# Layer 0 feed-forward by seven block products instead of eight, with narrower PSUM tiles and half-width modulation steps

## The chip, the cores and the metric

The kernel runs on one core of a Trainium2 chip. The metric is the device time of one execution in microseconds, median of several. The core's engines run side by side, each through its own list of instructions in program order: TensorE (PE, matrix products; its weight loads are shown apart as PEld), VectorE (DVE), ScalarE (ACT), GpSimd (POOL) and SyncE (SP, which here only issues transfers). An instruction starts when the one before it on its engine lets it and when what it waits for on other engines or transfers is done.

## The reference, cut to what matters

A two-layer block on 512 latent tokens and 256 context tokens (768 together) of width 1024. Both layers end in the same feed-forward part; its hidden width is 2816, 22 tiles of 128.

```
for i in range(2):
    mod_lat = split((silu_c  @ ada_w[i] + ada_b[i]), 6)     # six vectors of 1024 ("chapters")
    mod_ctx = split((silu_cc @ ada_w[i] + ada_b[i]), 6)
    ...mixer (layer 0: a gated linear recurrence; layer 1: attention over all tokens)...
    x   = x   + mod_lat[5] * swiglu(modulate(rmsnorm(x,   g), mod_lat[3], mod_lat[4]), w_in[i], w_out[i])
    ctx = ctx + mod_ctx[5] * swiglu(modulate(rmsnorm(ctx, g), mod_ctx[3], mod_ctx[4]), ...)   # layer 0 only

def swiglu(h, w_in, w_out):
    g, u = split(h @ w_in, 2)
    return (silu(g) * u) @ w_out
```

## The kernel before

Activations lie with features on the partitions: `hh`/`hl` hold the normalised input as 8 tiles ("k tiles") of 128 features by 768 tokens, latent first. Every matrix product runs three times, since each operand is a rounded high part and a low part (the rest): high·high, low·high, high·low, all into the same PSUM tile.

Weights come through the class `Stream`. SP loads raw tiles of up to 1 MB (two at a time); ACT copies each half of 1024 columns into a high part `wh`, and `low_engine` (DVE in the feed-forward) subtracts to get the low part `wl`. Four such units are kept ahead of TensorE; `st.done(unit)` frees one and lets the next be split.

Layer 0's feed-forward is `ffn(0, ...)`. It takes the 22 hidden tiles in three phases of 8, 8 and 6. For a hidden tile `j` it forms the gate product (`f..g`) and the input product (`f..u`), each over 8 k tiles, three matmuls per k tile, each of these cut into 512 latent and 256 context columns; then ACT takes silu of the gate into `sg`, DVE multiplies (`sg`), ACT and DVE split the result into `ah` and `al`. After a phase's tiles come 8 output tiles (`fo`), added into the residual `xT` by `residual`, one DVE instruction for the latent and one for the context columns. PSUM tiles are three of 1024 columns (`psm`, 2 banks each), from which everything takes turns. The first two tiles' products are interleaved with the norm (`entry`).

Beside it run the modulation steps of layer 1. `ada_step` takes one loaded tile of `ada_w` (128 x 1024, 512 KB, two buffers, loads issued on GpSimd's queue) and adds it on DVE, scaled by silu(c), to a running sum (`ada_sum`; chapters 0 and 1 also for the context, `adac`). After eight of them `ada_add` sums over partitions on TensorE with `pick`, ACT copies (`adasb`), TensorE transposes, DVE adds the bias. All six chapters (48 steps) are done in layer 0's feed-forward, one step after a gate product and one after each tile. `ada_until` does what is missing of a chapter at once.

`boundary` interleaves the last output tiles with the next norm and the first products of layer 1. Layer 1's feed-forward is the same function with 512 columns, and has no modulation steps left.

Of the kernel before, what the change touches and what calls it, by code (L numbers as in the profile page):

```python
# [61 lines left out]
class Stream:  # L62
# [16 lines left out]
    def unit(self, load, n, pieces):  # L79
        self.units.append((load, n, pieces))  # L80
        self.loads[load][2] += 1
        return len(self.units) - 1
# [9 lines left out]
    def advance(self, limit=1 << 30):  # L92
        nc = self.nc
        self.flush()
        while self.split < min(len(self.units), self.base + NB_W + sum(i >= self.base for i in self.more), limit):
            i = self.split
            load, n, pieces = self.units[i]
            raw = self.raw[load]
# [3 lines left out]
            for dst, src in pieces:  # L102
                nc.scalar.activation(dst(hi), src(raw), AF.Copy)  # L103
            self.tiles[i] = (hi, lo)
            self.split += 1
            self.pending.append(i)
            if len(self.pending) > 1:
                self._low(self.pending.pop(0))

    def _low(self, i):  # L110

        load, n, pieces = self.units[i]
        raw, (hi, lo) = self.raw[load], self.tiles[i]
        for dst, src in pieces:
            self.low_engine.tensor_tensor(dst(lo), src(raw), dst(hi).bitcast(F32), op=ALU.subtract)  # L115
        self.loads[load][2] -= 1
        if self.loads[load][2] == 0:
            del self.raw[load]
            self.fill()

    def flush(self):
        while self.pending:
            self._low(self.pending.pop(0))

    def get(self, i):
        if i in self.pending:
# [13 lines left out]
def kernel(ctx, tc, x, c, ctx_in, c_ctx, ada_w, ada_b, norm_mix_g, norm_ffn_g, ffn_w_in,  # L140
# [19 lines left out]
    psm = ctx.enter_context(tc.tile_pool(name="psm", bufs=3, space=bass.MemoryType.PSUM))  # L160
    psa = ctx.enter_context(tc.tile_pool(name="psa", bufs=1, space=bass.MemoryType.PSUM))
    psx = ctx.enter_context(tc.tile_pool(name="psx", bufs=1, space=bass.MemoryType.PSUM))

    def ps_main(name):
        return psm.tile([P, 1024], F32, name=name, tag="main")
# [40 lines left out]
    adas = [(l, ch, k) for l in range(2) for ch in range(6) for k in range(KT) if l or ch > 1]  # L206
    ada_tiles = {}
    ada_state = {"loaded": 0, "used": 0, "evac": None, "sums": None}

    def ada_fill(eng=nc.gpsimd):  # L210
        while ada_state["loaded"] < len(adas) and ada_state["loaded"] < ada_state["used"] + NB_ADA:
            i = ada_state["loaded"]
            l, ch, k = adas[i]
            t = ada_pool.tile([P, 1024], F32, name=f"ada{i}", tag="ada")
            eng.dma_start(t, ada_w[l, k * P:(k + 1) * P, ch * D:(ch + 1) * D])  # L215
# [94 lines left out]
    add_ffn(0)  # L310
# [84 lines left out]
    def ada0_evac(q):  # L395
        k0, w = PARTS0[q]
        n, r = 64 * w, slice(k0, k0 + w)
        sb = tmp.tile([P, 256], F32, name=f"ada0sb{q}", tag="adasb", bufs=1)
# [32 lines left out]
    def ada_sum(i, t, ch, k):  # L431

        if ch < 2:
# [1012 lines left out]
```

## Time and profile before

| | |
|---|---|
| time, median of 3 runs | 1587.01 us (1586.71 to 1588.82) |
| the profiled execution | 1590.76 us, of which the span is 1589.0 us |
| TensorE, matmul / weight load, share of the span | 97% / 83% |
| VectorE, ScalarE, GpSimd | 51%, 38%, 16% |
| mean granted TensorE clock | 0.986 of full speed |
| DMA | 155.09 MB, mean 98 GB/s |

The span is the profiled part of that execution; 1.76 us lie around it. An engine's share says how long it was busy, not that others waited for it. Layer 0's feed-forward goes from about 365 us to 938 us of the span, attention and the mixer's output after it to about 1210 us, layer 1's feed-forward to the end.

### The profile page before, as it was taken

To read this page: it belongs to the slowest core of one execution; us is meant where nothing else is said; L and a number is where in the kernel's file an instruction comes from. 1 tells how busy PE (TensorE), PEld (TensorE's weight loads), DVE (VectorE), ACT (ScalarE), POOL (GpSimd) and SP (SyncE) were. 2 spreads that over 40 slices of the span, in tenths; PEclk is the share of its full clock that TensorE was granted. 3 is DMA by queue.
4 is the path that set the end of the run, shared out by engine and by line. 5 is a ranking of instruction groups with operands and counts; after the bars stand their busy time and mean duration, and the time that the engine had idled before them with its cause. 6 is when DMAs were issued, how large, how long until landed. Compare 5 with 4: busy or idle time off the path is not lost.

```text
span 1589.0 us, 20937 instructions
## 1 busy us (share of the span) xinstructions
PE 1533.8 (97%) x8895; PEld 1321.7 (83%) x8895; DVE 810.3 (51%) x1068; ACT 603.0 (38%) x812; POOL 254.0 (16%) x213
## 2 busy tenths in 40 slices
PE   7999998979999999999999999999998999999998
PEld 5887877868888888888888977899998888888887
DVE  6665778686555433344332375656547333233234
ACT  5476555734222112121121333676644332232223
POOL 3233333341000000000000233111125000000002
PEclk9999999999999999999999999999999999999999
DMA  9334343230334433334321222110012223223222
GB/s 358 123 108 132 106 127 112 82 104 27 106 125 137 136 101 125 120 118 136 118 65 56 67 60 70 29 43 27 22 62 78 80 82 131 80 81 131 80 67 93
DMA packets 121405, 155.09 MB, mean 98 GB/s; under 512 B 5211, under 2 KB 104144, under 8 KB 121312
## 3 DMA queue, kind: packets, MB, share of 16 engines
q1 hardware_dynamic: 109456, 112.21, 21.8%
q0 software_dynamic: 11552, 41.02, 8.1%
q8 instruction: 70, 1.15, 0.3%
q10 hardware_dynamic: 304, 0.53, 0.1%
q14 instruction: 23, 0.19, 0.0%
HBM read 151.64 MB, written 2.10 MB: 97 GB/s over the span
## 4 chain that ended last, share of the span: by engine, by line
PE 81%; DVE 12%; ACT 4%; issue 3%; DMA 0%; POOL 0%; DVEq 0%; SPq 0%; ACTq 0%; POOLq 0%
PE fo L678 18%; PE f L678 14%; PE lo L678 3%; PE s L1245 3%; PE wo L678 2%; PE ga L678 2%; PE o L1287 2%; DVE yc L785 2%; DVE hl L564 1%; DVE tg L848 1%; PE t L1263 1%; PE u L678 1%; PE k L678 1%; PE ckv L678 1%; DVE tg L850 1%
## 5 line engine op out<-in xcount | busy, mean ns | idle before, releaser
L103 ACT ACTIVATE wh<-raw 128x1024 fp32r<-128x1024 f32 (+2 forms) x195 | 191.3, 1011 | 194.3 <-PE fo L678 154.5
L115 POOL TENSOR_TENSOR wl<-raw,wh 128x1024 fp32r<-128x1024 f32 (+3 forms) x66 | 155.2, 2361 | 326.7 <-ACT wh L103 319.9
L678 PE MATMUL fo<-ah,wh 128*128 128x512 f32 (+1 forms) x552 | 167.5, 348 | 0.0
L678 PE MATMUL fo<-ah,wl 128*128 128x512 f32 (+1 forms) x552 | 166.8, 347 | 0.0
L678 PE MATMUL fo<-al,wh 128*128 128x512 f32 (+1 forms) x552 | 166.5, 346 | 0.0
L115 DVE TENSOR_TENSOR wl<-raw,wh 128x1024 fp32r<-128x1024 f32 (+1 forms) x129 | 151.1, 1199 | 2.7 <-ACT wh L103 2.6
L672 POOL TENSOR_TENSOR acc<-acc,sq 128x256 f32<-128x256 f32 (+1 forms) x52 | 51.7, 995 | 487.9 <-ACT sq L670 480.5
L678 PE MATMUL f<-hh,wl 128*128 128x512 f32 x336 | 128.7, 387 | 0.0
L678 PE MATMUL f<-hl,wh 128*128 128x512 f32 x336 | 128.6, 387 | 0.0
L678 PE MATMUL f<-hh,wh 128*128 128x512 f32 x336 | 128.6, 387 | 0.0
L659 DVE SCALAR_TENSOR_TENSOR xT<-fo,mod,xT 128x512 f32<-128x512 f32 (+1 forms) x76 | 46.6, 635 | 153.9 <-PE fo L678 153.6
L215 POOL DMA_DIRECT2D ada<-in_ada_w_dram x78 | 41.9, 538 | 509.0 <-DVE ada L443 383.6
L998 ACT ACTIVATE ah<-sg 128x768 fp32r<-128x768 f32 (+1 forms) x44 | 32.5, 739 | 195.8 <-DVE sg L997 195.8
L678 PEld LDWEIGHTS fo<-ah,wh 128*128 128x128 f32 x552 | 93.4, 189 | 14.1 <-issue 0.4
L678 PEld LDWEIGHTS fo<-al,wh 128*128 128x128 f32 x552 | 93.4, 188 | 13.5
L678 PEld LDWEIGHTS fo<-ah,wl 128*128 128x128 f32 x552 | 93.2, 188 | 13.2
L997 DVE TENSOR_TENSOR sg<-sg,f 128x512 f32<-128x512 f32 (+1 forms) x21 | 14.7, 700 | 137.7 <-ACT sg L996 134.7
L678 PEld LDWEIGHTS f<-hh,wh 128*128 128x128 f32 x336 | 62.6, 188 | 13.0
L678 PEld LDWEIGHTS f<-hl,wh 128*128 128x128 f32 x336 | 62.5, 188 | 12.9
L678 PEld LDWEIGHTS f<-hh,wl 128*128 128x128 f32 x336 | 62.5, 188 | 12.7
L443 DVE SCALAR_TENSOR_TENSOR ada<-ada,csil,ada 128x1024 f32<-128x1024 f32 x42 | 53.8, 1282 | 33.1 <-DMA ada<-in_ada_w_dram 32.6
L996 ACT ACTIVATE sg<-f 128x512 f32<-128x512 f32 x20 | 11.9, 597 | 148.6 <-PE f L678 148.6
(657 smaller groups left out, 3475.7 us busy)
## 6 DMA issues: line engine op xcount, KB each, us to landing
raw<-in_ffn_w_in_dram SPq DMA_DIRECT2D x44, 1024.0 KB, 4.9
ada<-in_ada_w_dram POOLq DMA_DIRECT2D x78, 512.0 KB, 4.2
raw<-in_ffn_w_out_dram SPq DMA_DIRECT2D x16, 1024.0 KB, 4.9
ada<-in_ada_w_dram SPq DMA_DIRECT2D x32, 256.0 KB, 5.5
raw<-in_ffn_w_out_dram SPq DMA_DIRECT2D x8, 768.0 KB, 4.7
raw<-in_lru_w_in_dram SPq DMA_DIRECT2D x10, 512.0 KB, 5.3
raw<-in_lru_gate_w_dram SPq DMA_DIRECT2D x16, 256.0 KB, 3.1
raw<-in_lru_w_out_dram SPq DMA_DIRECT2D x8, 512.0 KB, 3.8
```

Source lines behind the costliest of these rows:

```text
L103: nc.scalar.activation(dst(hi), src(raw), AF.Copy)
L115: self.low_engine.tensor_tensor(dst(lo), src(raw), dst(hi).bitcast(F32), op=ALU.subtract)
L215: eng.dma_start(t, ada_w[l, k * P:(k + 1) * P, ch * D:(ch + 1) * D])
L443: dve.scalar_tensor_tensor(t, t, csil[:, k, 0:1], ada_ps["lat"], op0=ALU.mult, op1=ALU.add)
L564: return lambda: dve.scalar_tensor_tensor(hl[:, k, s], t[:, :n], mod[:, l, ch, v, k:k + 1], hh[:, k, s].bitcast(F32), op0=ALU.add, op1=ALU ...
L659: dve.scalar_tensor_tensor(xT[:, m, s], ps[:, s], mod[:, l, ch, v, m:m + 1], xT[:, m, s], op0=ALU.mult, op1=ALU.add)
L672: accs.append(lambda: nc.gpsimd.tensor_tensor(acc[:, s], acc[:, s], sq[:, s], op=ALU.add))
L678: pe.matmul(ps[:, off + s.start:off + s.stop], a, b[:, s], start=first and i == 0, stop=last and i == 2)
L785: dve.scalar_tensor_tensor(y[:, s0:s1], ps[:, s0 + o:s1 + o], convw(tap, k), y[:, s0:s1], op0=ALU.mult, op1=ALU.add)
L998: act.activation(ah[:, j, :n], sg[:, :n], AF.Copy)
L1245: pe.matmul(ps[:, o:o + 384], x, y[:, k0:k1], start=j == 0, stop=j == 4)
L1287: pe.matmul(ps[:, :256], x[:, t % 4, hs], y[:, t, :], start=t == 0 and j == 0, stop=t == NT - 1 and j == 2)
```

## The change

`ffn0` replaces `ffn(0)`. Tokens are cut into two halves of 384 (A and B), the 8 k tiles into two halves of four, and a hidden tile's gate and input columns are the two halves of the weight's columns. The product of a 2x2 by a 2x2 block matrix is then formed by seven block products (each 4 k tiles, three matmuls of 384 columns each) in place of eight: `product(p, j, ...)`. For that, four differences of blocks of the input are made once (`differences`, in four calls of one k tile), and four sums of weight blocks for each hidden tile (`sums`, `sum4`, on DVE, in the raw tile and two temporaries). The products' results are put together in PSUM, on ACT and on DVE (`pair`). The first three hidden tiles are still done in the old way (`plain`), while the differences are made; the other 19 by seven products. There are six phases ("chunks") of 4, 2, 4, 4, 4, 4 tiles, so the residual is added into `xT` six times. PSUM is laid out anew (`ps_layout`): six tiles of 512 columns behind the third hidden tile.

The modulation steps of layer 1 take tiles of 128 x 512 (three buffers), 96 in place of 48, with the running sum in `acc`. There is one in each pair, one or two behind an output tile, `ada_until(1, 4)` at the end of the last chunk for what is missing of chapters 0 to 4, and the sixteen of chapter 5 are moved into layer 1's feed-forward: three `ada_step()` in a row behind each hidden tile. The last chapter of layer 0 is asked for with `ada_until(0, 5)` where it was `(0, 4)`. The layer-1 part of `ffn` stays as it was but for these steps.

```diff
+    PAIRS0 = (4, 2, 4, 4, 4, 4)
+    PLAIN0 = 3
+    ORDER = (1, 5, 6, 2, 7, 3, 4)
...
+        def sums(j):
+            a11, a12, a21, a22 = (block(st.raw[loads[j]], a) for a in range(4))
+            s1, s2 = (sums_pool[0](f"s{j}{i}") for i in "12")
+            temps[j].update({5: s1, 6: s2})
+            dve.tensor_tensor(s1, a21, a22, op=ALU.add)
+            dve.tensor_tensor(a21, a11, a21, op=ALU.subtract)
+            dve.tensor_tensor(s2, a22, a21, op=ALU.subtract)
+        def sum4(j):
+            a12 = block(st.raw[loads[j]], 1)
+            dve.tensor_tensor(a12, a12, temps[j][6], op=ALU.subtract)
...
-        for j in range(4):
+        for j in range(2):
+            r = 64 * half + 32 * j
             for v, a in enumerate(sums):
-                pe.matmul(ps[32 * j:32 * j + 32, :256], pick[:, v, :], a[:, j * 256:(j + 1) * 256],
+                pe.matmul(ps[r:r + 32, :256], pick[:, v, :], a[:, j * 256:(j + 1) * 256],
                           start=v == 0, stop=v == len(sums) - 1)
-        ada_copy(i, 1, ch, ps)
+        if half == 1:
+            ada_copy(i, l, ch, ps)
...
                     ada_step()
+                    ada_step()
+                    ada_step()
                 if ph == 0:
-                    ada_until(l, 5)
+                    ada_until(1, 5)
...
+            def product(p, j, ps, first, last):
+                unit, h, _ = s0_units[j, p]
+                wh, wl = st.get(unit)
+                k0, xh, xl, s = ops7[p]
+                for k in range(4):
+                    o = h * 512 + k * P
+                    for q, (w, x) in enumerate(((wh, xh), (wh, xl), (wl, xh))):
+                        pe.matmul(ps, w[:, o:o + P], x[:, k0 + k, s], start=first and k == 0 and q == 0,
+                                  stop=last and k == 3 and q == 2, skip_group_check=not first)
...
+            def differences(kp):
...
+                for i in range(2):
+                    for y, s in zip(x[i], (A, B)):
+                        k = kp + 4 * i
+                        dve.tensor_tensor(y, hh[:, k, s].bitcast(F32), hl[:, k, s].bitcast(F32), op=ALU.add)
+                (a0, b0), (a1, b1) = x
+                dve.tensor_tensor(a0, b0, a0, op=ALU.subtract)
+                dve.tensor_tensor(b0, b1, b0, op=ALU.subtract)
+                dve.tensor_tensor(b1, b1, a0, op=ALU.subtract)
+                dve.tensor_tensor(a1, a1, b1, op=ALU.subtract)
+                f = (a0, b1, b0, a1)
...
+                for i in range(4):
+                    act.activation(dh[i][:, kp, :], f[i], AF.Copy)
+                for i in range(4):
+                    dve.tensor_tensor(dl[i][:, kp, :], f[i], dh[i][:, kp, :].bitcast(F32), op=ALU.subtract)
...
+            def pair(j, i):
+                g = tmp.tile([P, T], F32, name=f"g0{j}", tag="nt")
+                p5 = ptemp(f"p5{j}")
+                x, y, z = (ps_bank(f"{c}{j}")[:, :H2] for c in "xyz")
+                product(1, j, x, True, True)
+                act.activation(g[:, A], x, AF.Copy)
+                while split:
+                    split.pop()()
+                release(1, j)
+                product(5, j, z, True, True)
+                act.activation(p5, z, AF.Copy)
+                release(5, j)
+                product(6, j, x, False, True)
+                act.activation(g[:, B], x, AF.Copy)
+                release(6, j)
+                product(2, j, y, True, True)
+                dve.tensor_tensor(g[:, A], g[:, A], y, op=ALU.add)
+                act.activation(g[:, A], g[:, A], AF.Silu)
+                release(2, j)
+                ada_step()
+                product(7, j, x, False, True)
+                dve.tensor_tensor(p5, p5, x, op=ALU.add)
+                release(7, j)
+                product(3, j, z, False, True)
+                dve.tensor_tensor(g[:, B], g[:, B], z, op=ALU.add)
+                act.activation(g[:, B], g[:, B], AF.Silu)
+                release(3, j)
+                product(4, j, x, False, True)
+                dve.tensor_tensor(g[:, B], g[:, B], p5, op=ALU.mult)
+                dve.tensor_tensor(g[:, A], g[:, A], x, op=ALU.mult)
+                split.append(lambda: split_hidden(i, g))
+                release(4, j)
...
+            plain(0, made[0], made[2])
+            differences(0)
+            differences(1)
+            plain(1, made[1], None)
+            differences(2)
+            differences(3)
+            for j in range(2, PLAIN0):
+                plain(j, None, None)
+            ps_layout((6, 512))
+            for c, (h0, nh, outs) in enumerate(s0_out):
+                for j in range(max(h0, PLAIN0), h0 + nh):
+                    pair(j, j - h0)
...
+                if lastp:
+                    ada_until(1, 4)
...
+                two = [out_tile(c, m, (gb, ga), range(nh - 1)) for m in range(2)]
+                for m in range(KT):
+                    ps = out_tile(c, m, (gb, ga), (nh - 1,) if m < 2 else range(nh), two[m] if m < 2 else None)
+                    for g in (gb, ga):
+                        residual(m, lambda s: ps[g[0]], 0, 5, g, False)
+                    out_done(c, m)
+                    ada_step(1 if nh == 4 and not LATONLY() else 2 if nh == 4 else m % 2)
```

The first place is VectorE between the first hidden tiles of layer 0. Before, this stands behind the multiplication of the first tile (`sg` is the product of silu and input, `al` its low part, `wl` a weight's low part, `adac` and `ada` the sums of the modulation):

```order
L997 TENSOR_TENSOR sg_3368<-sg_3368,f00u 128x768
L999 TENSOR_TENSOR al_3167<-sg_3368,ah_3166 128x768
L115 TENSOR_TENSOR wl_3374<-raw_2945,wh_3373 128x1024
L436 TENSOR_SCALAR adac_3377<-ada_2623,csil 128x1024
L441 TENSOR_SCALAR ada_2623<-ada_2623,csil 128x1024
L997 TENSOR_TENSOR sg_3431<-sg_3431,f_3382 128x768
L999 TENSOR_TENSOR al_3167<-sg_3431,ah_3166 128x768
L115 TENSOR_TENSOR wl_3437<-raw_2945,wh_3436 128x1024
```

Now the four calls of `differences` stand there, two behind the first tile and two behind the second. The fourth, and what follows it, reads (`x30`, `x31` are its temporaries, `t0l` to `t2l` and `al0` the low parts of the differences, `g02` the third tile's multiplication):

```order
L1178 TENSOR_TENSOR x30_3537<-hh0_78,hl0_79 128x384 x2
L1178 TENSOR_TENSOR x31_3538<-hh0_78,hl0_79 128x384 x2
L1180 TENSOR_TENSOR x30_3537<-x30_3537 128x384
L1181 TENSOR_TENSOR x30_3537<-x31_3538,x30_3537 128x384
L1182 TENSOR_TENSOR x31_3538<-x31_3538,x30_3537 128x384
L1184 TENSOR_TENSOR x31_3538<-x31_3538 128x384
L1191 TENSOR_TENSOR t0l_3173<-x30_3537,t0h_3170 128x384
L1191 TENSOR_TENSOR t1l_3174<-x31_3538,t1h_3171 128x384
L1191 TENSOR_TENSOR t2l_3175<-x30_3537,t2h_3172 128x384
L1191 TENSOR_TENSOR al0_3169<-x31_3538,ah0_3168 128x384
L1262 CAST hl0_79<-al0_3169 128x4x384
L1265 TENSOR_TENSOR g02_3655<-g02_3655,f02u_3604 128x768
```

So 48 instructions of 384 columns and one of 1536 stand on VectorE ahead of the third tile's multiplication, which reads the last PSUM tile of the old layout; the first product of the fourth tile (`x3`, in the new layout) waits for that multiplication.

The second place is VectorE at the end of the last chunk. Now the steps of `ada_until(1, 4)` stand between the split of the last hidden tile (`al0`) and the first residual (`xT`):

```order
L1248 TENSOR_TENSOR g021_7445<-g021_7445,x21_7447 128x384
L119 TENSOR_TENSOR wl125_7535<-raw62_7466,wh125_7534 128x1024
L1195 TENSOR_TENSOR al0_3169<-g021_7445,ah0_3168 128x768
L537 SCALAR_TENSOR_TENSOR acc_229<-ada106_7256,csil_128,acc_229 128x512
L537 SCALAR_TENSOR_TENSOR acc_229<-ada107_7396,csil_128,acc_229 128x512
L537 SCALAR_TENSOR_TENSOR acc_229<-ada108_7516,csil_128,acc_229 128x512
L537 SCALAR_TENSOR_TENSOR acc_229<-ada109_7572,csil_128,acc_229 128x512
L537 SCALAR_TENSOR_TENSOR acc_229<-ada110_7575,csil_128,acc_229 128x512
L537 SCALAR_TENSOR_TENSOR acc_229<-ada111_7578,csil_128,acc_229 128x512
L522 TENSOR_TENSOR mod_143<-adax111_7586,cols_b_126 128x8 x2
```

Six steps stand there in one piece; TensorE's `pick` matmuls for this sum stand ahead of the last chunk's output tiles in its list.

The third place is layer 1's feed-forward behind its third hidden tile. Before, VectorE has there (`sg102` the tile's multiplication):

```order
L997 TENSOR_TENSOR sg102_10261<-sg102_10261,f102_10212 128x512
L999 TENSOR_TENSOR al10_9973<-sg102_10261,ah10_9972 128x512
L115 TENSOR_TENSOR wl133_10210<-raw83_9947,wh133_10209 128x1024
L115 TENSOR_TENSOR wl134_10270<-raw84_10206,wh134_10269 128x1024
L997 TENSOR_TENSOR sg103_10322<-sg103_10322,f103_10273 128x512
```

Now three modulation steps come behind the lows:

```order
L1101 TENSOR_TENSOR sg102_10919<-sg102_10919,f102_10870 128x512
L1103 TENSOR_TENSOR al10_10607<-sg102_10919,ah10_10606 128x512
L119 TENSOR_TENSOR wl160_10859<-raw83_10581,wh160_10858 128x1024
L119 TENSOR_TENSOR wl161_10928<-raw84_10855,wh161_10927 128x1024
L537 SCALAR_TENSOR_TENSOR acc_229<-ada118_10862,csil_128,acc_229 128x512
L537 SCALAR_TENSOR_TENSOR acc_229<-ada119_10865,csil_128,acc_229 128x512
L535 TENSOR_SCALAR acc_229<-ada120_10868,csil_128 128x512
```

And on TensorE the `pick` matmuls, which read the finished sum in `acc`, stand between this tile's last matmul and the next tile's first:

```order
L784 MATMUL f102_10870<-hl1_10400,wh159_10851 128x512
L784 MATMUL f102_10870<-hh1_10399,wl159_10852 128x512
L558 MATMUL psada119_10937<-acc_229,pick_130 32x256 x2
L784 MATMUL f103_10943<-hh1_10399,wh158_10848 128x512
L784 MATMUL f103_10943<-hl1_10400,wh158_10848 128x512
```

The same stands behind the sixth hidden tile, for the chapter's other half.

## Rows read from the trace of the kernel before

**Rows 1.** The page, part 1: busy time, share and instructions of each engine.
```profile
PE 1533.8 (97%) x8895; PEld 1321.7 (83%) x8895; DVE 810.3 (51%) x1068; ACT 603.0 (38%) x812; POOL 254.0 (16%) x213
```
**Rows 2.** Windows: length, busy of PE, PEld, DVE, ACT, POOL; clock, DMA share, GB/s.
```profile
500.00:600.00 100.00, 100.00 (x589) 86.62 (x588) 45.32 (x52) 16.27 (x18) 6.86 (x13) 1.00 0.41 130
```
**Rows 3.** Timeline of PE, layer 0 feed-forward: start, length, operation, tiles, shapes, count.
```profile
449.81 0.51 PE L678 MATMUL f004u<-hh,wh 128*128 128x512 f32 x2
...
451.89 0.39 PE L678 MATMUL f005g<-hh,wh 128*128 128x512 f32 x1
```
**Rows 4.** Timeline of PE in attention.
```profile
1100.00 0.51 PE L1245 MATMUL s<-kh,qh 128*128 128x384 f32 x2
...
1101.74 0.28 PE L1287 MATMUL o<-pth,vh 128*128 128x256 f32 x1
```
**Rows 5.** DVE groups by shape, 385 to 950 us: count | busy, mean ns | idle before.
```profile
L115 DVE TENSOR_TENSOR wl<-raw,wh 128x1024 fp32r<-128x1024 f32 x56 | 66.7, 1219 | 0.0
...
L999 DVE TENSOR_TENSOR al<-sg,ah 128x768 fp32r<-128x768 f32 x22 | 21.1, 958 | 20.1 <-ACT ah L998 20.1
L659 DVE SCALAR_TENSOR_TENSOR xT<-fo,mod,xT 128x512 f32<-128x512 f32 x24 | 18.0, 750 | 87.0 <-PE fo L678 87.0
...
L659 DVE SCALAR_TENSOR_TENSOR xT<-fo,mod,xT 128x256 f32<-128x256 f32 x24 | 11.4, 477 | 3.8 <-PE fo L678 3.7
```
**Rows 6.** Timeline of DVE in the first hidden tiles of layer 0.
```profile
392.34 0.95 DVE L997 TENSOR_TENSOR sg<-sg,f00u 128x768 f32<-128x768 f32 x1 [6.99 <-PE f00u L678]
...
395.16 1.22 DVE L115 TENSOR_TENSOR wl<-raw,wh 128x1024 fp32r<-128x1024 f32 x1
396.30 0.74 DVE L436 TENSOR_SCALAR adac<-ada,csil 128x1024 f32<-128x1024 f32 x1
...
417.84 0.95 DVE L997 TENSOR_TENSOR sg<-sg,f002u 128x768 f32<-128x768 f32 x1 [2.37 <-PE f002u L678]
```
**Rows 7.** ACT groups by shape, 385 to 950 us.
```profile
L998 ACT ACTIVATE ah<-sg 128x768 fp32r<-128x768 f32 x22 | 18.6, 846 | 179.2 <-DVE sg L997 179.2
...
L462 ACT ACTIVATE adasb<-psada 128x256 f32<-128x256 f32 x6 | 2.3, 382 | 25.3 <-PE psada L456 25.3
```
**Rows 8.** Timeline of DVE: two instructions of 1219 ns on average, in one row.
```profile
420.58 2.36 DVE L115 TENSOR_TENSOR wl<-raw,wh 128x1024 fp32r<-128x1024 f32 x2
```
**Rows 9.** Timeline of GpSimd's issues of modulation loads, and of DVE's use.
```profile
408.81 0.57 POOL L215 DMA_DIRECT2D ada<-in_ada_w_dram  x1 [44.43 <-DVE ada L443]
...
412.87 1.28 DVE L438 SCALAR_TENSOR_TENSOR adac<-ada,csil,adac 128x1024 f32<-128x1024 f32 x1 [3.18 <-DMA ada<-in_ada_w_dram]
```
**Rows 10.** Timeline of ACT and DVE in layer 1's feed-forward, two hidden tiles.
```profile
1250.61 0.60 ACT L996 ACTIVATE sg<-f 128x512 f32<-128x512 f32 x1 [6.11 <-PE f L678]
...
1253.24 2.35 DVE L115 TENSOR_TENSOR wl<-raw,wh 128x1024 fp32r<-128x1024 f32 x2
...
1261.49 0.60 ACT L996 ACTIVATE sg<-f 128x512 f32<-128x512 f32 x1 [7.94 <-PE f L678]
...
1264.46 2.36 DVE L115 TENSOR_TENSOR wl<-raw,wh 128x1024 fp32r<-128x1024 f32 x2 [0.26 <-ACT wh L103]
```
**Rows 11.** Timeline of PE: two places where it had been idle.
```profile
274.52 0.98 PE L678 MATMUL ga<-uh,wh 128*128 128x512 f32 x2 [5.05 <-DVE yc L785]
...
328.51 1.01 PE L678 MATMUL lo<-mh,wh 128*128 128x512 f32 x2 [8.20 <-DVE xT L659]
```
**Rows 12.** Windows behind these two places, columns as in rows 2.
```profile
276.00:280.00 4.00, 4.00 (x14) 3.42 (x14) 4.00 (x11) 2.44 (x3) 0.00 (x0) 0.50 0.00 0
280.00:282.00 2.00, 2.00 (x12) 1.69 (x12) 0.49 (x1) 0.41 (x1) 0.00 (x0) 0.95 0.04 8
...
328.00:330.00 2.00, 1.49 (x5) 1.30 (x6) 2.00 (x5) 0.00 (x0) 0.00 (x0) 0.50 0.01 4
330.00:332.00 2.00, 2.00 (x9) 1.73 (x9) 2.00 (x4) 0.55 (x1) 0.00 (x0) 0.65 0.00 0
```
**Rows 13.** The page, part 6: a weight load's size and landing.
```profile
raw<-in_ffn_w_in_dram SPq DMA_DIRECT2D x44, 1024.0 KB, 4.9
```

More of the change, by code (lines that the diff above doesn't have):

```diff
@@ L79, in unit, with mixed @@
     def unit(self, load, n, pieces):
-        self.units.append((load, n, pieces))
-        self.loads[load][2] += 1
+        return self.mixed([(load, dst, src, None, None) for dst, src in pieces])
+    def mixed(self, pieces):
+        self.units.append(pieces)
+        for load, *_ in pieces:
+            self.loads[load][2] += 1
         return len(self.units) - 1
@@ new lines, in strassen_units @@
+    def strassen_units(js):
+        loads = {j: strassen_load(j) for j in js}
+        temps = {j: {} for j in js}
+        block = lambda t, a: t[:, a * 512:(a + 1) * 512]
+        def sums(j):
[8 more added lines that the diff above has]
+            dve.tensor_tensor(a12, a12, temps[j][6], op=ALU.subtract)
+        raw_block = {1: 0, 2: 1, 3: 1, 7: 2, 4: 3}
+        seq = [(j, p) for j in js for p in ORDER]
+        for u in range(0, len(seq), 2):
+            pieces = []
+            for h, (j, p) in enumerate(seq[u:u + 2]):
+                dst = lambda t, h=h: t[:, h * 512:(h + 1) * 512]
+                if p in raw_block:
+                    src = lambda t, p=p: block(t, raw_block[p])
+                else:
+                    src = lambda t, j=j, p=p: temps[j][p]
+                pieces.append((loads[j], dst, src, (lambda j=j: sums(j)) if p == 1 else None,
+                               (lambda j=j: sum4(j)) if p == 2 else None))
+            i = st.mixed(pieces)
+            for h, (j, p) in enumerate(seq[u:u + 2]):
+                s0_units[j, p] = (i, h, h == len(pieces) - 1)
@@ L312 @@
+    add_ffn0()
     mla = {}
@@ L469, in ada_step @@
             i = ada_state["used"]
[L470 removed]
+            if i >= N_ADA[0]:
                 return
             ada_fill()
[L473 to L475 removed]
+            l, ch, k, *half = adas[i]
             t = ada_tiles.pop(i)
[L477 to L478 removed]
+            if half:
+                ada_sum(i, t, l, ch, k, *half)
             else:
@@ L490, in ada_until @@
     def ada_until(l, ch):
-        n = (l * 6 + ch - 1) * KT - ada_state["used"]
+        n = sum(1 for a in adas if a[:2] <= (l, ch)) - ada_state["used"]
         if n > 0:
```

257 lines of the change are left out of this document (192 added, 65 removed).

## The prediction

> **What bounds the kernel now.** I read the page's busy shares first, then a table of windows through layer 0's feed-forward, then single instructions. TensorE is busy 97% of the span [rows 1]. In a stretch of 100 us in the middle of the changed part it is busy without a break at the full clock, VectorE 45%, ScalarE 16% [rows 2]. So before, layer 0's feed-forward costs what its matmuls cost, and the other engines fit beside them. Fewer or shorter matmuls shorten it directly, until something on VectorE is late.
>
> **What the change takes away.** A hidden tile before is 2 products x 8 k tiles x 3 = 48 pairs of a 512- and a 256-column matmul. From 449.81 to 451.89 there are six pairs [rows 3]: 0.347 us a pair, 16.6 us a tile. Seven block products are 7 x 4 x 3 = 84 matmuls of 384 columns. Attention has such matmuls, each with its own weight load: ten from 1100.00 to 1101.74 [rows 4], 0.174 each, 14.6 us a tile. That saves 2.05 us (2.02 to 2.08) a tile, and 38.4 to 39.5 for 19 tiles: **39 us**. The output products have the same columns as before, in six chunks in place of three. A raw load of 1 MB, landing in 4.9 us [rows 13], is needed once a tile as before.
>
> **What it adds**, by the place where TensorE would wait.
>
> *A, the start.* The price of a 384-column VectorE instruction is not in the trace. Plain ones take 0.958 us for 768 columns and 1.219 for 1024 [rows 5], so about 1.02 ns a column, and 0.57 us for 384; two plain ones of 1.219 stand in 2.36 [rows 8], so the next begins 0.08 before the end and the pitch is 0.49. One call of `differences` has 12 of them, some of which need the result of the one before: I take 6.2 us (5.9 if they only queue, 6.8 without the overlap). VectorE multiplies the first tile at 392.34 and ends the next low at 396.4 [rows 6]; two modulation instructions, 0.8 together at half the width of the 0.74 there, make it 397.2. Two calls end at 409.6. Behind them stand the second tile's multiplication and low, 0.95 each, with 0.9 between them for the copy on ScalarE (0.846 [rows 7]): 412.4; three weight sums of 512 columns (0.70 each): 414.5; and only then the low `wl37` (1.2), which the third tile's input product reads: 415.7. Before, that product was over at 417.8, where the multiplication of `f002u` begins [rows 6]; it takes 8.3 us, so it should read this low at about 409.5 and idles 6 us. It is done at 424. VectorE meanwhile does three lows of 512 (2.0), two modulation steps (1.5), and two more calls: 431.6; the copy of 1536 columns (1.3) and the third multiplication (0.95) end at 433.9. Only this frees the PSUM for the fourth tile, whose first matmul would otherwise start at 417.8. **+16 us** (13 to 20), as two idles of 6 and 10 us.
>
> By the Trainium skill (VectorE: DVE Perf Modes, "The DRAIN you can't avoid") the next VectorE instruction does not start until the pipe is empty, so the 0.08 of overlap would not be there. By that rule A would be some 4 us longer; the trace's row differs from it, and I go by the row.
>
> *B, within the pairs.* Product 4 accumulates into the PSUM tile that product 7 left and VectorE's addition for `p5` reads. Between the ends of products 2 and 7 plus product 3, that is in 24 matmuls or 4.17 us, VectorE must do the gate's addition (0.57), two lows (0.70 each), a wait of about 0.6 for ScalarE, the fourth sum (0.70), one or two modulation instructions (0.75 each, taken from 512 columns [rows 5]) and the addition (0.57). In pairs of the other parity a low stands elsewhere and it fits. With two modulation instructions (chapters 0 and 1; four such pairs) it is 5.3 us: 1.1 late, 0.6 to 1.2. With one (five such pairs) 4.6: 0 to 0.5. **+5 us** (1 to 10).
>
> *C, end of the last chunk.* The partition sum, ahead of all output tiles on TensorE, waits for six steps. When the last product ends, VectorE has a multiplication (0.57), a low (1.22) and the low of the tile (0.96, with its wait) before the steps. Three loads are there; the other three are issued as buffers come free. From issue to use such a load took 4.06 us, 408.81 to 412.87, at 512 KB [rows 9]; now it has 256. The first step ends at 0.75, its buffer's load is in at 4.8, two more follow at 0.75, the last step ends at about 7.1. With the ScalarE copy (0.38 [rows 7], 0.7 with hand-overs) ahead of the transposes that is **+10 us** (8.5 to 11).
>
> *D, layer 1.* Twice the partition sum stands directly behind a hidden tile's last matmul, and its last step behind that tile's VectorE work. From the start of silu, which is when the tile's products end, to the end of the two lows it takes 1250.61 to 1255.59, 5.0 us, or 1261.49 to 1266.82, 5.3 us [rows 10]. Behind the one kind of tile stand two steps, behind the other one, of 0.75: 6.5 and 6.1. TensorE has nothing else: **+12.6 us** (12 to 13.5).
>
> *E, the clock.* After an idle of 5.05 us TensorE started at 274.52 [rows 11] and had the lower clock (1.2 of 2.4 GHz, 0.50) until about 280.2 (0.95 granted in 280 to 282 [rows 12]), so it lost 2.8 us. After 8.20 us of idle it started at 328.51 and had the lower level to about 331.4 (0.65 in 330 to 332 [rows 12]), a loss of 1.4. A has two such idles, C one, D two: five at 1.4 is **+7 us** (2, if some fall away or lie in a wait, to 14). B's short idles are costed without this.
>
> *F.* Two transposes stand directly behind their partition sum and wait for the copy [rows 7]: **+1.4** (0.7 to 1.5).
>
> The doubled residual instructions (24 more of 0.75 and of 0.48 [rows 5]) lie beside output products and cost nothing while VectorE has time there; it is idle some 55% of that stretch [rows 2]. The chapter of layer 0 asked for earlier was already done by then.
>
> Sum: 16 + 5 + 10 + 12.6 + 7 + 1.4 = 52, less 39: **+13 us**. With all bounds together it is -2 to +32. On the profiled execution's 1590.8 that gives 1603.8; the median of the runs lies 3.8 lower, so **1600 us**.
>
> **Rivals.**
>
> 1. *The other engines hide all of it.* VectorE is idle 55% [rows 2], and the gain of 39 is all that is left: 1548. For it speaks that average. Against it: each of A, C and D is a wait of TensorE for a named instruction that in VectorE's own order cannot be earlier, whatever the average; VectorE's work does not shorten by being off the bound before. The Trainium skill (Perfetto Trace Analysis, "Identifying the Most-Contended Engine") says to optimise the engine of highest occupancy first, which for TensorE is to be judged by its weight loads' busy share; by that rule, at 86.6 against 45.3 [rows 2], the change attacks the right engine and this rival is its result. 0.04.
>
> 2. *Narrow VectorE instructions are much cheaper* (the side on which it is faster). If the pitch at 384 columns were p in place of 0.49, A falls by 48 x (0.49 - p) and B nearly goes. At p = 0.25 that is 11.5 and 4.5, so -3: 1584. It decides from p = 0.30 or so, where the sum is about 0. Against it: 256 columns took 0.477 and 512 took 0.750 in the residual's instructions [rows 5], a line that gives 0.61 for 384. With idles that don't cost the clock it needs only p = 0.40. 0.13 for all ways to end near or under zero.
>
> 3. *VectorE becomes the bound of the pairs.* A pair gives it seven lows (4.9), four sums (2.8), three additions and two multiplications (2.85), the tile's low (0.96) and one or two steps (0.75 each): 12.3 to 13.0 of 14.6 us. Waits for ScalarE of a microsecond or two, like the 0.85 of that copy [rows 7], fill the rest. Each microsecond beyond is 19 in all. With 0.6 in all pairs on average: 1612. 0.15.
>
> 4. *384 columns do not hide the weight load in layer 0*, so that a block product runs at 0.19 a matmul: 16.0 a tile, a gain of 13 and not 39: 1626. Against it: attention's ten in a row, each with its load [rows 4]. 0.03.
>
> **How the numbers follow.** My forecast has 0.65 (its own range 1592 to 1613). Of rival 2, 0.07 end faster by over 0.2% (3.2 us, about what a measurement can tell from no change) and 0.06 within it. Faster: 0.04 + 0.07 = 0.11. Same: 0.06, and 0.01 of the forecast's lower edge, 0.07. Slower: 0.82. The range of 8 in 10 leaves out rival 1, half of rival 2, rival 4 and a third of rival 3, about 0.19: 1588 to 1616.
>
> **What would show it.** Gain: `x`, `y`, `z` matmuls of 384 columns at 0.174, 14.6 us a pair. A: TensorE idle about 6 us before the third tile's matmul with `wl37`, and about 10 before the first `x3`, released by VectorE. B: about 1 us before product 4 in some pairs, released by the `p5` addition. C: about 10 us before the `psada` of the last chunk. D: two idles of about 6 us before `psada` in layer 1's feed-forward. E: a granted clock of 0.5 behind each. I am wrong if VectorE's 384-column instructions are far from 0.5, if TensorE's idles in the pairs sum to far more than 5 us, or if a load, not VectorE, ends one of these waits.

## The result and the profile after

The changed kernel takes 1623.08 us (median of 4 runs, 1622.39 to 1625.06) against 1587.69 for the kernel before in the same job: ratio 1.0225, 95% interval 1.0207 to 1.0242, 35 us slower. The forecast was slower, 1600, with 1616 as the upper end: the sign is right, the time lies outside the range, and the loss is nearly three times the forecast's 13.

The profiled execution has a span of 1620.6 us, against 1589.0. The page's busy times of the changed kernel:

```profile
PE 1516.2 (94%) x8667; PEld 1330.2 (82%) x8667; DVE 980.1 (60%) x1474; ACT 679.8 (42%) x998; POOL 282.0 (17%) x261
```

TensorE has 228 recorded matmuls fewer and is busy 94% of the span, where it was 97% [rows 1]. The windows of the changed kernel: the 100 us of [rows 2], then all of layer 0's feed-forward, then the first phase of layer 1's.

```profile
500.00:600.00 100.00, 95.74 (x539) 90.53 (x538) 73.69 (x117) 37.40 (x64) 4.84 (x9) 0.98 0.32 98
356.00:946.00 590.00, 545.52 (x3032) 501.08 (x3030) 413.88 (x672) 200.35 (x343) 65.98 (x99) 0.96 0.31 94
1253.00:1337.00 84.00, 71.29 (x302) 56.84 (x301) 31.39 (x39) 19.28 (x26) 5.74 (x11) 0.92 0.34 115
```

VectorE went from 45% to 74% in these 100 us, which is not full. TensorE is idle for 44.5 us of layer 0's part and 12.7 of layer 1's phase, and the mean granted clock is 0.96 and 0.92. So there are two losses: idles, and a lower clock behind them.

The gain is there as computed. In the timeline of TensorE, the first and last matmul of one block product, and the first of the next:

```profile
535.72 0.33 PE L1160 MATMUL z<-t0h,wh 128*128 128x384 f32 x1
...
537.62 0.33 PE L1160 MATMUL z<-t0h,wl 128*128 128x384 f32 x1
537.80 0.33 PE L1160 MATMUL x<-t1h,wh 128*128 128x384 f32 x1
```

Twelve matmuls in 2.08 us, 0.1733 each: 14.6 us a pair, as [rows 4] gave it. The waits of TensorE in the changed kernel (by whom, us in total, times, longest):

```profile
PE psada L558 <- DVE acc L537: 26.5, 5, 9.2
...
PE x L1160 <- DVE g L1265: 7.4, 1, 7.4
PE psada L558 <- DVE ada L542: 5.5, 3, 3.7
PE adax L519 <- ACT acc L565: 4.0, 3, 2.8
PE x L1160 <- DVE p L1240: 3.7, 4, 0.9
...
PE f02u L784 <- ACT wh L108: 2.9, 1, 2.9
...
PE f02u L784 <- DVE wl L119: 2.2, 1, 2.2
...
PE fo L1206 <- ACT ah L1194: 1.6, 1, 1.6
```

The reader sees that 36 of these 54 us are waits of the modulation (`psada`, `adax`), not of the seven products. One by one, `psada` and `adax` in the timeline of TensorE, layer 0 and then layer 1:

```profile
610.94 1.07 PE L558 MATMUL psada<-ada,pick 128*32 128x256 f32 x4 [3.75 <-DVE ada L542]
...
716.06 1.07 PE L558 MATMUL psada<-acc,pick 128*32 128x256 f32 x4 [2.97 <-DVE acc L537]
...
806.92 0.62 PE L558 MATMUL psada<-acc,pick 128*32 128x256 f32 x4 [1.61 <-DVE acc L537]
...
827.76 0.69 PE L519 MATMUL adax<-ident,acc 128*128 128x128 f32 x2 [2.82 <-ACT acc L565]
...
906.91 1.07 PE L558 MATMUL psada<-acc,pick 128*32 128x256 f32 x4 [9.24 <-DVE acc L537]
908.47 0.69 PE L519 MATMUL adax<-ident,acc 128*128 128x128 f32 x2 [0.48 <-ACT acc L565]
...
1270.73 1.07 PE L558 MATMUL psada<-acc,pick 128*32 128x256 f32 x4 [6.58 <-DVE acc L537]
...
1312.29 1.07 PE L558 MATMUL psada<-acc,pick 128*32 128x256 f32 x4 [6.13 <-DVE acc L537]
```

The last three waits of `psada` were forecast (9.2, 6.6 and 6.1 us for 10, 6.5 and 6.1). The first three were not: they stand among the out tiles of the chunks, and two smaller ones, of 1.54 and 0.26, stand there too. In the kernel before none of layer 1's six partition sums waits. There a gate product of some 8 us lies on TensorE between the last step and the sum; among the out tiles it is now at most one out tile, of some 4 us. One of the six:

```profile
596.22 0.64 PE L456 MATMUL psada<-ada,pick 128*32 128x256 f32 x8
```

What VectorE does in the changed kernel ahead of the wait of 3.75 us, in its timeline:

```profile
604.42 1.14 DVE L760 SCALAR_TENSOR_TENSOR xT<-fo,mod,xT 128x512 f32<-128x512 f32 x2
605.47 1.22 DVE L119 TENSOR_TENSOR wl<-raw,wh 128x1024 fp32r<-128x1024 f32 x1
606.60 0.69 DVE L365 TENSOR_TENSOR s<-raw 128x512 f32<-128x512 f32 x1
...
608.66 0.69 DVE L119 TENSOR_TENSOR wl<-raw,wh 128x512 fp32r<-128x512 f32 x1
609.26 0.75 DVE L537 SCALAR_TENSOR_TENSOR acc<-ada,csil,acc 128x512 f32<-128x512 f32 x1
610.04 0.75 DVE L542 SCALAR_TENSOR_TENSOR ada<-ada,csil,ada 128x512 f32<-128x512 f32 x1
```

An out tile's step comes behind its residual and, at every second tile, behind the lows and weight sums for the next hidden tile; the `psada` matmuls need the step's result and are next on TensorE. VectorE was idle for 4.49 us before its residual at 601.91. It is not short of time in this stretch; it comes too late to the one instruction that is waited for.

Around and behind each longer idle of this execution the granted clock is at its lower level, 1.2 of 2.4 GHz. There are nine such stretches in the changed parts, beside one at the norm, around 365 us, which the kernel before has too. Four of the nine, and the sum over all (length, then busy times, clock):

```profile
609.30:616.10 6.80, 5.16 (x18) 3.49 (x19) 3.48 (x7) 0.00 (x0) 1.08 (x2) 0.50 0.66 187
715.10:721.90 6.80, 5.84 (x19) 4.38 (x20) 4.16 (x7) 0.00 (x0) 1.61 (x3) 0.50 0.49 149
...
902.90:913.00 10.10, 5.60 (x25) 4.72 (x26) 3.94 (x9) 0.80 (x2) 0.54 (x1) 0.50 0.21 73
1268.10:1274.80 6.70, 4.07 (x11) 2.67 (x12) 3.03 (x4) 0.00 (x0) 1.61 (x3) 0.50 0.78 265
...
sum 57.20, PE 39.34 PEld 30.93 DVE 33.55 ACT 8.65 POOL 6.46; mean PE 4.37 PEld 3.44 DVE 3.73 ACT 0.96 POOL 0.72
```

TensorE worked 39.3 us at half the clock there, so by estimate some 20 us are lost by it, half of that time. How many of the shorter idles bring such a stretch differs from execution to execution (see behind e4).

### The profile page after: what moved, and what is told of

It reads as the page before. It is cut to its first block, busy times and chain, and to the rows that moved or that the text cites. A ratio compares the mean times of both kernels' runs of the same rounds, so it can differ in the third digit from the quotient of the medians.

```text
span 1620.6 us, 21238 instructions
## 1 busy us (share of the span) xinstructions
PE 1516.2 (94%) x8667; PEld 1330.2 (82%) x8667; DVE 980.1 (60%) x1474; ACT 679.8 (42%) x998; POOL 282.0 (17%) x261
## 4 chain that ended last, share of the span: by engine, by line
PE 63%; issue 15%; DVE 15%; ACT 4%; DMA 1%; POOL 1%; SPq 0%; DVEq 0%; POOLq 0%; ACTq 0%
PE f L784 14%; PE fo L784 7%; PE fo L1206 6%; PE x L1160 4%; PE lo L784 3%; PE s L1536 3%; PE ga L784 2%; PE wo L784 2%; PE o L1578 2%; PE z L1160 2%; PE p L784 2%; PE g L784 2%; DVE yc L892 1%; PE t L1554 1%; PE y L1160 1%
## 5 line engine op out<-in xcount | busy, mean ns | idle before, releaser
L108 ACT ACTIVATE wh<-raw 128x1024 fp32r<-128x1024 f32 (+3 forms) x250 | 209.6, 865 | 215.7 <-PE fo L1206 63.5
L119 DVE TENSOR_TENSOR wl<-raw,wh 128x1024 fp32r<-128x1024 f32 (+2 forms) x184 | 170.4, 938 | 11.9 <-ACT wh L108 11.8
L760 DVE SCALAR_TENSOR_TENSOR xT<-fo,mod,xT 128x512 f32<-128x512 f32 (+1 forms) x124 | 74.3, 626 | 129.3 <-PE fo L1206 65.7
L239 POOL DMA_DIRECT2D ada<-in_ada_w_dram x96 | 51.7, 539 | 559.3 <-DVE ada L542 280.8
L1206 PE MATMUL fo<-ah,wh 128*128 128x512 f32 (+1 forms) x352 | 100.2, 352 | 1.6 <-ACT ah L1194 1.6
L1101 DVE TENSOR_TENSOR sg<-sg,f 128x512 f32<-128x512 f32 x20 | 13.8, 688 | 142.1 <-ACT sg L1100 142.1
L1206 PE MATMUL fo<-al,wh 128*128 128x512 f32 (+1 forms) x352 | 98.6, 347 | 0.6 <-DVE al L1195 0.6
L1206 PE MATMUL fo<-ah,wl 128*128 128x512 f32 (+1 forms) x352 | 98.0, 345 | 0.0
L784 PE MATMUL fo<-ah,wh 128*128 128x512 f32 (+1 forms) x200 | 72.9, 364 | 0.0
L784 PE MATMUL fo<-ah,wl 128*128 128x512 f32 (+1 forms) x200 | 72.7, 364 | 0.0
L784 PE MATMUL fo<-al,wh 128*128 128x512 f32 (+1 forms) x200 | 72.7, 364 | 0.0
L784 PEld LDWEIGHTS f<-hl,wh 128*128 128x128 f32 x320 | 60.8, 190 | 12.6
L1206 PEld LDWEIGHTS fo<-ah,wh 128*128 128x128 f32 x352 | 59.4, 198 | 11.9 <-issue 2.9
L537 DVE SCALAR_TENSOR_TENSOR acc<-ada,csil,acc 128x512 f32<-128x512 f32 x84 | 62.8, 747 | 6.5 <-DMA ada<-in_ada_w_dram 5.6
```

Source lines behind the costliest of these rows:

```text
L108: nc.scalar.activation(dst(hi), src(self.raw[load]), AF.Copy)
L119: self.low_engine.tensor_tensor(dst(lo), src(self.raw[load]), dst(hi).bitcast(F32), op=ALU.subtract)
L239: eng.dma_start(t, ada_w[l, k * P:(k + 1) * P, c0:c0 + 512])
L537: dve.scalar_tensor_tensor(first, t, csil[:, k, int(both):int(both) + 1], first, op0=ALU.mult, op1=ALU.add)
L760: dve.scalar_tensor_tensor(xT[:, m, s], ps(s) if callable(ps) else ps[:, s], mod[:, l, ch, v, m:m + 1], xT[:, m, s], op0=ALU.mult, op1=ALU ...
L784: pe.matmul(ps[:, off + s.start:off + s.stop], a, b[:, s], start=first and i == 0, stop=last and i == 2)
```

## Experiments

The theory after reading the trace: each wait is local, it stands where TensorE's program puts a small matmul directly behind the VectorE (or ScalarE) instruction that it needs, and it costs its idle time and a stretch at the lower clock. The rivals: VectorE has become the bound and a wait that is removed comes back at the next place; or the lower clock has another cause. All ratios are to the kernel before in the same job; the changed kernel's own is 1.0225.

**e1: the out tiles' partition sums later.** `ada_step` takes nothing up until a finished sum is a place or two old. One out tile counts as a place, a pair as two; where lows stand ahead, one more. The four out tiles of the second chunk that had no step get one, so that six steps stay for the end, as before.

```diff
         for _ in range(n):
-            ada_evac(n == 1)
+            if spread[0]:
+                if ada_state["evac"] and ada_state["place"] >= ada_state["copied"]:
+                    ada_evac()
+                if ada_state["sums"] and ada_state["place"] < ada_state["ready"]:
+                    return
+            else:
+                ada_evac(n == 1)
             ada_add()
...
-                    ada_step(1 if nh == 4 and not LATONLY() else 2 if nh == 4 else m % 2)
+                    ada_place(1, m % 2)
+                    ada_step(1 if nh == 4 and not LATONLY() else 2 if nh == 4 else 1)
```

> The changed kernel with the partition sums of layer 1's modulation (`psada`) and their transposes put off by one or two out tiles in layer 0, so that TensorE does not come to them directly behind the VectorE step that they need; the burst of six steps at the end of the last chunk is kept. In the changed kernel's trace these waits are 1.54, 0.26, 3.75, 2.97, 1.61 us before `psada` and 0.67, 2.82 before the transposes, 13.6 together, and the stretches of out tiles hold about 9 us of matmuls at the lower clock. Theory (each wait is local, and each costs its idle time and a stretch of lower clock behind it): 1623 falls by about 20, to 1603, ratio to the kernel before 1.010. Rival (VectorE has no room in these stretches, so that the wait only moves to the next place that needs it): at most 5 less, 1618, ratio 1.019.

Measured: 1606.52, ratio 1.0112 (1.0098 to 1.0126). That is 16.6 less than the changed kernel, not the full 20: two `psada` waits are left, one of 1.61 us as in the changed kernel, and one of 1.38 in the second chunk, where the changed kernel has 0.26. The waits of 3.75, 2.97 and 2.82 are gone and none of that size took their place, so 10.6 of the 13.6 us of idle went. The lower clock is granted once instead of four times among the out tiles, which is not all the edit's doing (see behind e4). The sums' waits for `acc` (with the last chunk's 9.4, and layer 1's two) and for `ada` are now these:

```profile
PE psada L560 <- DVE acc L538: 23.7, 4, 9.4
...
PE psada L560 <- DVE ada L543: 1.4, 1, 1.4
```

So the unforeseen idle sat here, and it is a matter of order.

**e2 and e8: layer 1's steps spread.** e2:

```diff
                         prod(pg, gu, hh, hl, sl)
+                        ada_step()
                         prod(pu, uu, hh, hl, sl, off=off)
...
                         pu, off = pg, SEQ
+                        ada_step()
                         prod(pu, uu, hh, hl, sl, off=off)
...
-                    ada_step()
-                    ada_step()
-                    ada_step()
+                    ada_step(1 if j or ph else 5)
```

> The changed kernel with layer 1's sixteen modulation steps spread: five behind the first hidden tile, then one between gate and input product and one behind each tile, so that the partition sums stand a whole product behind their last step. The two idles there are 6.58 and 6.13 us, and 5.1 us more are lost in that phase to matmuls at the lower clock. Theory (idle and clock both come back): 17.8 less, 1605, ratio 1.011. Rival (the lower clock has nothing to do with these waits): 12.7 less, 1610, ratio 1.0145. If VectorE could not do the steps beside its other work there, a new wait would show behind them.

Measured: 1610.48, 1.0138 (1.0125 to 1.0152), 5 us short of the expected. The partition sums wait no more, but five steps in a row behind the first tile do. VectorE's timeline in e2:

```profile
1248.37 1.54 DVE L537 SCALAR_TENSOR_TENSOR acc<-ada,csil,acc 128x512 f32<-128x512 f32 x2
1251.59 0.75 DVE L537 SCALAR_TENSOR_TENSOR acc<-ada,csil,acc 128x512 f32<-128x512 f32 x1 [1.69 <-DMA ada<-in_ada_w_dram]
1253.58 1.54 DVE L537 SCALAR_TENSOR_TENSOR acc<-ada,csil,acc 128x512 f32<-128x512 f32 x2 [1.24 <-DMA ada<-in_ada_w_dram]
```

There are three buffers; the fourth and fifth step wait for loads, and everything behind them on VectorE with them. TensorE then waited 2.2 us for a weight and ran at the lower clock behind it. e8 has at most three in a row:

```diff
-                    ada_step(1 if j or ph else 5)
+                    for _ in range(3 if ph == 0 and j < 2 else 1):
+                        ada_step()
```

> The kernel of e2 with three steps behind each of the first two hidden tiles in place of five behind the first. In e2 (1610.5, where 1605 was expected) the fourth and fifth step waited 1.69 and 1.24 us for their loads, the second tile's weights came late on ScalarE and VectorE, and TensorE waited 2.5 us and ran at the lower clock behind it. Theory (that is the whole shortfall): 1605, ratio 1.011. Rival (the steps don't fit beside the feed-forward's own VectorE work): 1610 as e2.

Measured: 1606.67, 1.0102 (1.0086 to 1.0118); the expected 1.011 lies in the interval. The phase itself, from its first `f` matmul behind the entry to its first `fo`, takes 69.6 us, against 73.0 in e2, 83.5 in the changed kernel and 65.3 in the kernel before. So 13.9 of its 18.2 us of loss come back, with no stretch at the lower clock left in it; one `psada` wait of 1.68 us stays.

**e3: the first call of `differences` early.**

```diff
-            plain(0, made[0], made[2])
             differences(0)
+            plain(0, made[0], made[2])
             differences(1)
```

> The changed kernel with the first of the four calls of `differences` put ahead of the first hidden tile's multiplication on VectorE, where the trace shows it idle for 6.99 us; everything else as it was. Theory (the start is bound by the length of VectorE's row of work, 387 to 428 us): the wait before `x3` falls from 7.4 to about 1.5 us, 6 less and 1 to 3 less for the clock: 1615, ratio 1.017. Rival (the start waits for weight copies on ScalarE or for loads as much as for VectorE): within 2 us of the changed kernel, 1622.

Measured: 1614.33, 1.0162 (1.0148 to 1.0176), 8.7 less. VectorE's row of work does set the start: from layer 0's first gate product to the first output tile of the second chunk it takes 150.4 us in place of 154.9. But the wait went elsewhere than I wrote: both waits before `f02u` are gone (2.9 and 2.2), one of 0.9 before `f01u` is new, and that before `x3` is 8.6 where 1.5 was expected, since the third tile now ends earlier and VectorE's fourth call still stands ahead of the multiplication.

```profile
PE x L1160 <- DVE g L1265: 8.6, 1, 8.6
```

That the total came out at the expected 1615 is in part luck. Only those 4.4 us are gained at the start; the out tiles, which the edit leaves as they were, have one stretch at the lower clock in this execution in place of four (see behind e4).

**e4: work in place of idle.** 27 matmuls of 512 columns ahead of layer 1's two partition sums (`fill` is a PSUM tile, `h` the input).

```diff
         ada_state["sums"] = None
+        if ch == 5:
+            fill = ps_aux(f"fill{i}")
+            for _ in range(FILL):
+                pe.matmul(fill, ada_state["h"][:, 0, :P], ada_state["h"][:, 0, :512], start=True, stop=True)
```

> The changed kernel with 27 matmuls of 512 columns (6.2 us at 0.23 each, on data that is there, into a PSUM tile that nothing reads) ahead of each of the two partition sums of layer 1, so that TensorE works where it waited 6.58 and 6.13 us. Nothing gets shorter by it. Theory (the lower clock follows the idle): both stretches of lower clock in that phase are gone and their 5.1 us come back, 1618, ratio 1.019. Rival (the lower clock has another cause, or costs nothing while TensorE is behind VectorE anyway): no change, 1623, ratio 1.0225.

Measured: 1620.39, 1.0197 (1.0183 to 1.0211), 0.0028 below the changed kernel with 54 matmuls more. The expected 1.019 lies in the interval and the rival's 1.0225 does not, but it just touches the changed kernel's interval, so the phase itself has to decide. The windows in e4, around the two places and over the phase:

```profile
1266.00:1276.00 10.00, 9.53 (x44) 7.25 (x43) 5.55 (x7) 2.18 (x3) 1.62 (x3) 1.00 0.48 166
1306.00:1316.00 10.00, 9.98 (x46) 7.63 (x45) 4.41 (x5) 4.47 (x6) 0.00 (x0) 1.00 0.33 105
1255.00:1335.00 80.00, 79.51 (x354) 64.53 (x353) 31.39 (x39) 19.17 (x25) 5.92 (x11) 1.00 0.36 121
```

The full clock throughout, where the changed kernel had a mean of 0.92. From the phase's first `f` matmul behind the entry to its first `fo` it took 80.0 us (1255.4 to 1335.3), against 83.5 (1253.1 to 1336.6), and 82.7 to 83.4 in e1, e3, e5 and e6, which keep both waits. At these two places the lower clock follows from the idle, and it costs some 2 us behind each. That is 3.5 together and not the expected 5.1; half of the 7.6 us of matmuls at the lower clock there would be 3.8.

What the shorter idles cost is less settled. In the out tiles of layer 0 the program of e2, e4 and e8 is the changed kernel's, with the same waits to 0.1 us. Ten us around the wait of 2.97 in the changed kernel, and around the same wait in e4 (2.86) and in e8 (2.96):

```profile
712.70:722.70 10.00, 7.03 (x26) 5.17 (x25) 5.66 (x10) 1.15 (x2) 2.69 (x5) 0.66 0.57 171
715.60:725.60 10.00, 7.14 (x42) 5.66 (x41) 7.41 (x13) 1.15 (x2) 2.69 (x5) 1.00 0.60 171
714.50:724.50 10.00, 7.04 (x27) 5.18 (x26) 5.83 (x10) 1.15 (x2) 2.69 (x6) 0.66 0.62 180
```

TensorE starts 42 matmuls in e4 and 26 in the changed kernel, after the same idle. Of the four stretches at the lower clock among the out tiles e8 has all, and e2, e3 and e4 have one, of some 3.4 us behind the wait of 3.75. From its first gate product to its last output tile, layer 0's feed-forward takes 589.0 us in the changed kernel, 589.2 in e8, 582.5 in e2 and 584.4 in e4. So 5 to 7 us of the profiled loss come and go without an edit, and what decides it stays open. Idles of 6.1 us and more in the two feed-forward parts brought the lower clock in every execution traced.

**e5: no burst at the end.** e1, and in the pairs:

```diff
                 release(4, j)
+                if LATONLY():
+                    ada_step()
```

> The kernel of e1 (1606.5) with one more modulation step in each pair of the last three chunks, so that no step is left for the end of the last chunk. Theory (the wait of 9.4 us before the last chunk's output tiles is these six steps and their loads): about 3 us of it stay, for the last hidden tile's own multiplication and low; 6.5 us of idle and 2 to 3 for the clock come back, 1597, ratio 1.006. Rival (VectorE is full in the pairs, and an additional step there makes a product late): 1602 or more, with waits before product 4 in the last three chunks.

Measured: 1597.32, 1.0046 (1.0031 to 1.0062), 9 less than e1. Less than expected stays of the wait: 0.70 and 0.61 us, for the last tile's high and low part. No wait before product 4 shows in the last three chunks, so the rival falls there.

**e6: the step behind `p5`.** In `pair`, `ada_step()` moves from behind product 2 to behind the addition into `p5`.

> The changed kernel with the modulation step of a pair put behind the addition for `p5` in place of ahead of it. Theory (that addition, which product 4 waits for, stands behind the step's one or two instructions): the four waits of 0.92 us go, 3.7 less, 1619.4, ratio 1.020. Rival (the lows ahead of it make the addition late): no change, 1623, ratio 1.0225.

Measured: 1619.65, 1.0187 (1.0173 to 1.0202); the expected 1.020 lies in the interval. The four waits of 0.92 are gone. But the wait for `ah` before the first output tile of the second chunk, 1.6 us in the changed kernel, got longer:

```profile
PE fo L1206 <- ACT ah L1194: 2.7, 1, 2.7
```

**e7: all of it.** e5, e3, e6 and e8 in one kernel.

> All together: partition sums put off (e1), no burst (e5), first call of the differences early (e3), the step behind `p5` (e6), and layer 1's steps spread with three behind each of the first two hidden tiles and no more than that in a row. Theory (the waits are local and add up): 1606.5 less 9 (burst), 8.7 (start), 3.2 (p5) and 17 (layer 1): 1568, ratio 0.987, which is faster than the kernel before by nearly half of the 39 us that the seven products save; what stays of the loss is the start's wait of some 8 us, the last chunk's 3 and the sums' own matmuls. Rival (VectorE is at its limit, and waits removed at one place come back at another): over 1580.

Measured: 1574.27, ratio 0.99 (0.9887 to 0.9914): 1% faster than the kernel before, and 3% faster than the changed one, with the same products and the same modulation steps. It is 6 us more than expected. About 4 of these are e3's: all its 8.7 went into the sum, of which 4.4 are the start's. And the longer wait for `ah` of e6 is here too, so about 1 us did come back elsewhere. Its longest waits in the changed part:

```profile
PE x L1176 <- DVE g L1284: 9.0, 1, 9.0
...
PE fo L1222 <- ACT ah L1210: 3.4, 2, 2.7
PE psada L560 <- DVE acc L538: 3.2, 2, 1.7
```

The start keeps 9 us, with 10 us at the lower clock around it. The windows of e7 over layer 0's feed-forward:

```profile
356.00:909.00 553.00, 532.90 (x3027) 494.07 (x3026) 411.83 (x672) 199.91 (x343) 65.20 (x99) 0.98 0.33 100
```

TensorE is idle for 20.1 us in place of 44.5, with the same 412 us of VectorE work (411.8 and 413.9) in 37 us less: the rival that VectorE is the bound falls.

## Why the prediction was wrong

By its own terms, predicted against the changed kernel's trace, in us:

| term | predicted | measured |
|---|---|---|
| gain of the seven products | 39 | 39 (14.6 a pair) |
| A, start | 16 | 12.5 (2.91 + 2.19 + 7.39) |
| B, before product 4 | 5 | 3.7 (4 x 0.92) |
| C, end of the last chunk | 10 | 9.7 (9.24 + 0.48) |
| D, layer 1 | 12.6 | 12.7 (6.58 + 6.13) |
| E, clock | 7 | about 20 in this execution (10.9 behind the five idles forecast, 8.8 behind others) |
| F, transposes | 1.4 | 3.5 (0.67 + 2.82) |
| `psada` among the out tiles | none | 10.1 (1.54 + 0.26 + 3.75 + 2.97 + 1.61) |
| first out tile of the second chunk | none | 2.2 (1.57 + 0.58) |

The losses add up to 74, less 39: 35. The span grew by 31.6; layer 0's and layer 1's feed-forward alone grew by 38, while stretches that the change doesn't touch came out some 6 shorter in this execution. The 3 us between 35 and 38 were not traced to a place.

**Right:** the direction, the gain, and A to D, each at the place and with the releaser named, but for 2.91 us of A. Those end with a weight copy on ScalarE, which stands there behind a copy that waits for VectorE, and e3, which moves VectorE's work alone, takes them away. A came out 3.5 lower. A call of `differences` took 6.0 us for the estimated 6.2, and the cast 0.96 where I took 1.3, which is 1.2 in all. The rest is that TensorE worked 1 us between the two waits before `f02u`, and came later to `x3` because it ran at the lower clock on the way, which E counts. The price of narrow VectorE work was the largest unknown, and the line through two wider shapes gave it well (0.55 for an estimated 0.57). Rival 2, which needed a pitch of 0.30 to 0.40, falls with these rows, the low parts of one call:

```profile
396.43 0.55 DVE L1191 TENSOR_TENSOR t0l<-x,t0h 128x384 fp32r<-128x384 f32 x1
396.90 0.55 DVE L1191 TENSOR_TENSOR t1l<-x,t1h 128x384 fp32r<-128x384 f32 x1
397.37 0.55 DVE L1191 TENSOR_TENSOR t2l<-x,t2h 128x384 fp32r<-128x384 f32 x1
```

A new one starts each 0.47 us, 0.08 before the end of the one before it, as in [rows 8]. By the Trainium skill's drain rule (VectorE: DVE Perf Modes, "The DRAIN you can't avoid"), as the prediction took it, the pitch would be 0.55. These rows don't bear that out. The same paragraph there ends with an exception that the prediction left out: a next operation that is not held starts earlier.

**Wrong, first: E.** "Five at 1.4" counted A, C and D alone, and took the lower of its two rows, 1.4 and 2.8; at their mean it would have been 10.5. The five cost 1.8 to 2.8 each by the windows' busy times, 10.9 together. Nine stretches at the lower clock followed and not five; the other four stand behind waits that I had not listed and cost 8.8. Among the out tiles, idles of 2.97 and 3.75 us were each answered by 6.8 us at the lower level, though I had priced only idles of 5 us and more. e2, e3 and e4 show that most of these 8.8 can also be absent with the same idles. e4 shows that at the two places in layer 1 the clock doesn't fall when TensorE is kept busy.

**Wrong, second: that the out tiles have no wait.** The sum has no term for the partition sums that stand among layer 0's out tiles. The step was the sentence that the doubled residuals "cost nothing while VectorE has time there; it is idle some 55%", with F as the only loss beside them. It argued from an average. I read TensorE's list against VectorE's order at the start, the end and in layer 1, and not in the out tiles, where the same pattern stands: `psada` directly behind a step, and the step behind residuals, lows and weight sums. By the table the idle at these places is 14.4 us more than forecast (10.1, 2.2 and 2.1 of F). With the 12.7 by which E was too small, less the 5 by which A to D were too large, that makes the 22 that the forecast missed. e1 took 16.6 away, some 11 of it as idle.

**The rivals.** That the other engines hide all (1548) falls: TensorE waits 54 us for them. The Trainium skill (Perfetto Trace Analysis, "Identifying the Most-Contended Engine") says to optimise the engine of highest occupancy first. The trace agrees in so far as e7, with most of the waits taken away, is faster than before. That VectorE bounds the pairs (1612) falls too: the four pairs of the last chunk took 59.5 us together, 14.9 each (838.0 to 897.5, with a partition sum among them), and e5 adds a step to such pairs and gets faster. The 384-column matmuls at 0.19 (1626) come near the measured time by chance: the pitch is 0.173.

## What to carry to other kernels

When small work is spread over a kernel's stages, read at every place where TensorE takes up its result what stands ahead of the producing instruction on its engine; the distance between producer and consumer in the program decides, not the engine's average load. Price an idle of TensorE at its length and the stretch at the lower clock behind it, and give that second price a range. Here 54 us of idle brought another 20 in the execution profiled, 5 to 7 less in others with the same idles, and the same work in another order (e7) turned 35 us of loss into 15 of gain.

## What was not expected of the hardware

In the changed kernel's trace, idles of 2.82 to 3.75 us among the out tiles were enough for stretches at the lower clock (0.50) of 3.3 to 6.8 us behind or around them, and one of 1.57 us with another of 0.58 close behind it for 3.3 us; single idles of 1.54 and 1.61 us there and those of 0.92 showed none. The same program gave the same stretches in e8. In e2 and e4 the idles of 2.82 and 2.86 to 2.93 us, and that of 1.57 with 0.58, showed none, and the one of 3.75 us only some 3.4 us. So the length of such an idle alone does not tell whether the clock falls.

Work that gives nothing made a phase shorter: 54 matmuls of 512 columns in two waits brought it from 83.5 to 80 us (e4).
